# An attention kernel on one core: the identity for the first transposes made on Pool instead of loaded, and Pool's loads gated by another row

## The chip, the cores and the metric

The kernel runs on one core of a Trainium2 chip. The time is in device microseconds of that core; the number compared is the median of several executions. A profile is one more execution, taken with the hardware profiler.

The engines are named as in the profile: PE is TensorE's matmul, PEld its weight load, DVE is VectorE, ACT ScalarE, POOL GpSimd, SP SyncE. A name with a q (ACTq, SPq) is the engine's sequencer, which issues DMAs. Loads issued from SP and ACT go through one DMA queue each (q1 and q10 in the profile), loads issued from Pool through q0; all of them share the core's 16 DMA engines.

## The reference

Plain attention over 8 batches, sequence length 2048, width 512, in float32:

```python
def reference(q, k, v):
    d_k = q.shape[-1]
    scores = np.matmul(q, k.transpose(0, 2, 1)) / np.sqrt(d_k)
    attn_weights = special.softmax(scores, axis=-1).astype(np.float32)
    return np.matmul(attn_weights, v)
```

## The kernel before

The kernel computes scores transposed (keys on the partitions, 512 queries side by side), takes their exponentials into float16 and multiplies these with V; a column of ones behind V gives the row sums. Most products run through a seven-product scheme for 2x2 blocks (Q and K sums on DVE, PE accumulating in PSUM); the scheme's steps are written out by hand as word lists, one word an action, in `SEQUENCES` and `OPENING`. Each engine executes its instructions in the order in which the program names them. Batch 0 is the only one whose loads nothing hides, and the change touches only its opening.

**Rows and chunks.** Q and K of a batch are 16 rows of 128x512 (a row: 128 positions on the partitions), in four chunks of four rows. Their transposes (width on the partitions) are needed as PE operands. For batch 0 most are made on PE against an identity, `nc.tensor.transpose(..., ident)` in `transposed` (L156); a DVE or ACT copy then takes the result from PSUM (L159). Later chunks and batches use DMA transposes from SP (L146).

**The first chunk.** `load_first` (L131) loads each of the first four rows of Q and of K by itself, in float32, into space that is used for other things later (`rows`, `cz`). The queues, in order of issue: SP takes Q row 0, Q row 1, K row 1, Q row 2, K row 2, Q row 3, K row 3; ACT takes K row 0, behind the identity's load (L95). `round_first` (L135) casts each row to float16, Q rows on DVE, K rows on ACT. `first_transpose` then transposes one row on PE, and DVE copies it. `piece` (L258) multiplies what is there already. `idle` (L768) issues dummy products on a zeroed tile named `warm` (it lies in `vt2`; L709 zeroes it on DVE), which keep PE running between them.

PE's order in the opening is: 6 dummies of 512 columns; transposes of Q row 0; 2 dummies; transposes of Q row 1; 4 dummies of 128 columns; transposes of K row 0; 6 dummies of 128 columns; the first piece (K row 0 with Q row 0); transposes of K row 1; a piece; transposes of Q row 2; and so on. DVE's order is: cast and copy of Q row 0, cast and copy of Q row 1, copy of K row 0, cast of Q row 2, copy of K row 1, and so on.

**The identity.** `ident` is a 128x128 corner of the tile `vt4`, which the V sums overwrite later. Before the change it is an array in DRAM, loaded by the first instruction on ACT's queue.

**Pool.** Pool sets two columns of ones (L710, L711), then copies one column of a landed row into a tile named `gate` (L728). That copy has no use but to hold back what stands behind it on Pool: ten loads, which cast to float16 on the way. They are the other three chunks of Q and K and the four chunks of V, in this order, the first two in two halves each:

```python
LOADS = 'q1 k1 q2 k2 k3 v0 v1 q3 v2 v3'
```

The chunks k1, k2 and k3 are transposed on PE in `OPENING` (words k10s, k12v, k20v, k22s, k30s, k32s), q1 in q10v and q12v; q2 by a DMA transpose on SP (L146), which waits for q2's load.

Of the kernel before, what the change touches and what calls it, by code (L numbers as in the profile page):

```python
# [12 lines left out]
def kernel(  # L13
# [21 lines left out]
    nc = tc.nc  # L35
    P = 128
# [54 lines left out]
    vt4 = const.tile([P, NJ, H], F16, name="vt4")  # L91
    ident = vt4[:, NJ - 1, 0:P]
    warm = vt2[:, 0:2, :].rearrange("p j d -> p (j d)")
    ident_dram = nc.inline_tensor(np.eye(P, dtype=np.float16), name="attn_identity")
    nc.scalar.dma_start(out=ident, in_=ident_dram.ap())  # L95
    NK = NJ // 2
    Q = H // 2
    vus = [[const.tile([P, NK, Q], F16, name=f"vu{n}_{h}") for n in (1, 2, 4)] for h in range(2)]
# [25 lines left out]
    firsts = {}  # L124
# [582 lines left out]
    )  # L707

    nc.vector.memset(warm, 0.0)  # L709
    nc.gpsimd.memset(vt1[:, :, H:H + 1], 1.0)  # L710
    nc.gpsimd.memset(vraw[0][:, :, 1, D:D + 1], 1.0)  # L711

# [12 lines left out]
        load_first("k", n, nc.sync, rest[n])  # L725

    gate = const.tile([P, 1], F32)
    nc.gpsimd.tensor_copy(out=gate[:], in_=firsts["k", 0][:, 0:1])  # L728

    new_p(1)  # L730
    spare = [
# [153 lines left out]
```

## Time and profile before

| | us |
|---|---|
| median of 3 runs | 788.87 |
| lowest, highest | 788.74, 789.52 |
| the profiled execution | 790.05 |
| its span | 788.2 |

The profiled execution is one more run; its own time stands 1.2 us over the median, and its span leaves 1.8 us around it. The page's second part cuts the span into 40 equal slices (19.7 us each):

```profile
## 2 busy tenths in 40 slices
PE   8999999999999999999999999999999999999998
...
DVE  5799988989889898998879988799897988889884
ACT  4888788787877878878787878878788777887762
POOL 4011100011000110010100001000110001100000
...
DMA  9999895889958889589895989958898688921113
```

Each digit is a tenth of busy time. PE is full but for the first and the last slice; the DMA engines are full in the first slices and have room after that.

In the lists that follow, a row of the timeline gives start and length in us, engine, line, operation, tiles (out<-in), shapes and, in brackets, how long the engine had been idle and what ended that. The chain of waits gives start, length and what, followed back from the last instruction. A DMA row gives the tiles, the issuing queue, the KB and the time from issue to landing.

### The profile page before, as it was taken

The numbers are of one execution on the slowest core, as the hardware profiler recorded it, in microseconds if no ns is written. First come the engines' busy times: TensorE is split into PE (matmuls) and PEld (weight loads), VectorE is DVE, ScalarE is ACT, GpSimd is POOL, SyncE is SP. The second block draws the span as 40 slices with busy tenths as digits, with TensorE's granted clock in tenths as the row PEclk, the third lists the DMA queues.
The fourth block names the chain that finished last, engine by engine and source line by source line (L and its number), as shares of the span: only waits on it lengthen the run. The fifth ranks groups of instructions, "written<-read, shape, count | busy, mean of one in ns | idle before, by whom it ended". The sixth has DMA issues, their size and how long they took to land.

```text
span 788.2 us, 16289 instructions
## 1 busy us (share of the span) xinstructions
PE 782.7 (99%) x6284; PEld 536.4 (68%) x6284; DVE 683.8 (87%) x1452; ACT 609.8 (77%) x1140; POOL 72.3 (9%) x105
## 2 busy tenths in 40 slices
PE   8999999999999999999999999999999999999998
PEld 6566667667667666666666666666666766766677
DVE  5799988989889898998879988799897988889884
ACT  4888788787877878878787878878788777887762
POOL 4011100011000110010100001000110001100000
PEclk9999999999999999999999999999999999999999
DMA  9999895889958889589895989958898688921113
GB/s 210 190 155 167 155 182 125 164 149 151 198 114 162 156 150 175 110 162 179 119 193 126 160 161 146 191 108 169 141 191 155 117 178 137 191 75 45 48 67 110
DMA packets 187789, 115.90 MB, mean 147 GB/s; under 512 B 121536, under 2 KB 170816, under 8 KB 187712
## 3 DMA queue, kind: packets, MB, share of 16 engines
q0 software_dynamic: 49664, 49.29, 43.7%
q1 hardware_dynamic: 137616, 65.22, 36.8%
q8 instruction: 49, 0.80, 0.4%
q10 hardware_dynamic: 432, 0.36, 0.2%
q14 instruction: 28, 0.23, 0.1%
HBM read 100.70 MB, written 33.55 MB: 170 GB/s over the span
## 4 chain that ended last, share of the span: by engine, by line
PE 97%; DMA 2%; DVE 0%; ACT 0%; issue 0%; ACTq 0%; DVEq 0%
PE t L298 46%; PE t L494 36%; PE t L418 12%; DMA kraw<-stage 1%; PE t L243 1%; PE t L258 1%; PE tr L156 1%; DMA rows<-in_k_dram 1%; PE t L566 0%; DVE kraw L159 0%; ACT rows L435 0%; DVE rows L506 0%; DVE ks L185 0%; ACT stage L135 0%; DVE cz L318 0%
## 5 line engine op out<-in xcount | busy, mean ns | idle before, releaser
L298 PE MATMUL t<-qraw,kraw 128*128 128x512 f16 x732 | 192.4, 379 | 0.0
L494 PEld LDWEIGHTS <-s 128*128 128x128 f16 x1536 | 147.8, 98 | 39.4 <-ACT rows L503 0.3
L298 PEld LDWEIGHTS <-kraw 128*128 128x128 f16 x984 | 93.3, 98 | 79.0 <-issue 0.2
L298 PE MATMUL t<-qs,ks 128*128 128x512 f16 x492 | 141.1, 379 | 0.0
L494 PE MATMUL t<-vt,s 128*128 128x257 f16 (+1 forms) x1024 | 132.9, 273 | 0.0
L237 ACT ACTIVATE right<-cz 128x1024 f16<-128x1024 f32 x123 | 129.9, 1056 | 0.3 <-DVE cz L318 0.3
L426 DVE TENSOR_TENSOR rows<-t,rows 128x256 f32<-128x256 f32 x210 | 88.1, 419 | 22.3 <-ACT rows L517 11.8
L298 PEld LDWEIGHTS <-ks 128*128 128x128 f16 x738 | 69.3, 98 | 46.7 <-issue 0.2
L503 ACT ACTIVATE rows<-t,scales 128x256 f32<-128x256 f32 x136 | 63.9, 471 | 45.2 <-PE t L494 20.9
L506 DVE SCALAR_TENSOR_TENSOR rows<-t,scales,rows 128x256 f32<-128x256 f32 (+1 forms) x134 | 64.0, 479 | 34.4 <-ACT rows L503 21.0
L321 DVE TENSOR_TENSOR cz<-t,cz 128x512 f32<-128x512 f32 x123 | 84.2, 685 | 10.5 <-ACT cz L315 7.9
L237 ACT ACTIVATE left<-t 128x512 f16<-128x512 f32 x128 | 76.5, 598 | 20.1 <-PE t L298 16.3
L237 ACT ACTIVATE right<-t 128x512 f16<-128x512 f32 x138 | 83.1, 605 | 8.5 <-PE t L298 5.7
L318 DVE TENSOR_TENSOR cz<-t,cz 128x512 f32<-128x512 f32 x123 | 84.2, 684 | 4.4 <-PE t L298 3.8
L312 ACT COPY cz<-t 128x512 f32<-128x512 f32 x122 | 71.4, 585 | 15.7 <-PE t L298 13.5
L315 ACT COPY cz<-t 128x512 f32<-128x512 f32 x123 | 71.6, 582 | 10.3 <-PE t L298 10.0
L418 PEld LDWEIGHTS <-left 128*128 128x128 f16 x960 | 62.3, 98 | 23.3 <-DVE left L398 4.1
L308 ACT COPY t<-t 128x512 f32<-128x512 f32 x121 | 69.8, 577 | 6.3 <-PE t L298 4.0
L298 PE MATMUL t<-qraw,ks 128*128 128x512 f16 x246 | 73.2, 379 | 0.0
L298 PE MATMUL t<-qs,kraw 128*128 128x512 f16 x246 | 73.2, 379 | 0.0
L494 PE MATMUL t<-vh,right 128*128 128x256 f16 x544 | 69.8, 273 | 0.0
L494 PE MATMUL t<-vh,s 128*128 128x257 f16 x512 | 66.7, 273 | 0.1
(87 smaller groups left out, 1067.1 us busy)
## 6 DMA issues: line engine op xcount, KB each, us to landing
out_dram<-rows SPq DMA_DIRECT2D x60, 512.0 KB, 3.4
vh<-in_v_dram POOLq DMA_DIRECT2D x32, 512.0 KB, 10.8
stage<-in_q_dram POOLq DMA_DIRECT2D x28, 512.0 KB, 6.5
stage<-in_k_dram POOLq DMA_DIRECT2D x28, 512.0 KB, 7.2
right<-in_k_dram POOLq DMA_DIRECT2D x2, 512.0 KB, 12.1
out_dram<-rows SPq DMA_DIRECT2D x4, 256.0 KB, 2.0
out_dram<-rows SPq DMA_DIRECT2D x7, 128.0 KB, 1.7
rows<-in_q_dram SPq DMA_DIRECT2D x2, 256.0 KB, 3.3
```

Source lines behind the costliest of these rows:

```text
L237: nc.scalar.activation(out=out_, in_=in_, func=EXP, scale=inv_sqrt_d)
L298: nc.tensor.matmul(dst[:], lhs[:, j, dc, :], rhs[:, :, dc, :], start=(n in (1, 5) and dc == 0), stop=(dc == 1), skip_group_check=True,)
L308: self.edges[0](out=self.y[:], in_=self.x[:])
L312: self.edges[1](out=self.cz[:, 1, :], in_=self.z[:])
L315: nc.scalar.copy(out=self.cz[:, 0, :], in_=self.x[:])
L318: nc.vector.tensor_add(self.cz[:, 1, :], self.x[:], self.cz[:, 1, :])
L321: nc.vector.tensor_add(self.cz[:, 0, :], self.z[:], self.cz[:, 0, :])
L418: nc.tensor.matmul(to, lhs[:, j, h, :], rhs[:, j, :], start=(n in (1, 2) and h == 0 and j == 0), stop=(j == NK - 1), skip_group_check=True,)
L426: nc.vector.tensor_add(acc, part, acc)
L494: nc.tensor.matmul(dst[:, 0:width], lhs(j), rhs(j), start=(first and j == 0), stop=(j == NJ - 1), skip_group_check=True,)
L503: nc.scalar.activation(out=out_, in_=src, func=COPY, scale=r)
L506: nc.vector.scalar_tensor_tensor(out=out_, in0=src, scalar=r, in1=out_, op0=MULT, op1=ADD)
```

## The change

The array in DRAM and its load on ACT's queue go. Pool makes the identity instead: a memset of the 128x128 corner to zero, and a select on the index (partition minus column), which keeps the zero where the index is not zero and fills in 1 where it is. Both stand on Pool ahead of the two columns of ones, and so ahead of the gate. The gate copy reads K row 1 instead of K row 0, and so waits for that row's landing.

```diff
-    ident_dram = nc.inline_tensor(np.eye(P, dtype=np.float16), name="attn_identity")
-    nc.scalar.dma_start(out=ident, in_=ident_dram.ap())
...
     nc.vector.memset(warm, 0.0)
+    nc.gpsimd.memset(ident, 0.0)
+    nc.gpsimd.affine_select(
+        out=ident, in_=ident, compare_op=mybir.AluOpType.not_equal, fill=1.0,
+        base=0, pattern=[[-1, P]], channel_multiplier=1,
+    )
     nc.gpsimd.memset(vt1[:, :, H:H + 1], 1.0)
     nc.gpsimd.memset(vraw[0][:, :, 1, D:D + 1], 1.0)
...
     gate = const.tile([P, 1], F32)
-    nc.gpsimd.tensor_copy(out=gate[:], in_=firsts["k", 0][:, 0:1])
+    nc.gpsimd.tensor_copy(out=gate[:], in_=firsts["k", 1][:, 0:1])
```

## The prediction

> **What bounds the kernel now.** I read the page's busy times first, then the chain of work that ended last in its first 13 us, then who waits for whom on PE.
>
> ```profile
> span 788.2 us, 16289 instructions
> PE 782.7 (99%) x6284; PEld 536.4 (68%) x6284; DVE 683.8 (87%) x1452; ACT 609.8 (77%) x1140; POOL 72.3 (9%) x105
> ```
>
> PE is busy for 782.7 of 788.2 us, so anything that no PE instruction waits for is worth nothing. The list of PE's waits over the whole span has three entries:
>
> ```profile
> PE t L768 <- DVE vt L709: 1.2, 1, 1.2
> PE tr L156 <- ACT stage L135: 0.6, 1, 0.6
> PE t L258 <- DVE kraw L159: 0.2, 1, 0.2
> ```
>
> All lie in the opening. The chain shows what set their end (start, length, what):
>
> ```profile
> ...
> 1.13 5.24 DMA rows<-in_k_dram
> 6.37 0.02 issue
> 6.39 0.63 ACT stage L135
> 7.02 0.05 issue
> 7.07 0.41 PE tr L156 x4
> 7.48 0.02 issue
> 7.50 0.44 DVE kraw L159
> 7.94 0.05 issue
> 7.98 0.40 PE t L258 x4
> 8.38 0.24 PE tr L156 x4
> 8.62 0.02 issue
> 8.64 0.43 DVE kraw L159
> 9.08 0.05 issue
> 9.12 0.61 PE t L258 x4
> ```
>
> The transfer of K row 0, issued at 1.13, lands at 6.37; then come its cast on ACT and its transposes on PE. Behind 9.12 the chain is PE pieces without a pause. So this change is worth what it moves the PE stream at 9.12 by, and whatever a later load then takes back.
>
> **What is removed.** The timeline of the opening (start, length, what; in brackets the idle time before and what ended it):
>
> ```profile
> 0.73 0.37 ACTq L95 DMA_DIRECT2D vt<-attn_identity  x1
> 0.74 0.87 SPq L131 DMA_DIRECT2D rows<-in_q_dram  x2
> 1.13 0.48 ACTq L131 DMA_DIRECT2D rows<-in_k_dram  x1
> 1.66 0.42 SPq L131 DMA_DIRECT2D rows<-in_k_dram  x1
> 3.58 0.43 DVE L135 CAST stage<-rows 128x512 f16<-128x512 f32 x1 [2.45 <-DMA rows<-in_q_dram]
> 4.06 0.61 PE L156 MATMUL tr<-vt,stage 128*128 128x128 f16 x4
> 7.07 0.40 PE L156 MATMUL tr<-vt,stage 128*128 128x128 f16 x4 [0.63 <-ACT stage L135]
> ```
>
> and the landing of K row 1, from the DMA issues (KB each, us from issue to landing):
>
> ```profile
> rows<-in_k_dram SPq DMA_DIRECT2D x1, 256.0 KB, 4.9
> ```
>
> Without the identity K row 0 is issued at 0.73 instead of 1.13, 0.40 earlier, and its queue no longer has 32 KB of identity ahead of it. Q row 0, on SP's queue, takes 2.8 us from issue (0.74) to its cast (3.58), K row 0 takes 5.24. If K row 0 takes anything from 2.8 to 4.9 us (the time of K row 1), it lands between 3.5 and 5.6, is cast by 6.3 at the latest, and PE no longer waits for it: the 0.63 us of idle time before 7.07 is the most that can be won here. The 0.2 us for DVE behind it stays: it is the copy of the transposed row.
>
> **What is paid for it.** The row then competes with Q row 0, and Q row 0 starts a chain too: its cast at 3.58, its transposes at 4.06, a copy, Q row 1's cast, transposes and copy, and then, in PE's order, K row 0's transposes. Each tenth by which Q row 0 lands later takes a tenth from the 0.63. Stages of the opening (PE, PEld, DVE, ACT, POOL busy; granted clock, DMA share, GB/s):
>
> ```profile
> 2.00:2.50 0.50, 0.50 (x3) 0.21 (x2) 0.00 (x0) 0.50 (x1) 0.00 (x0) 1.00 0.39 130
> 2.50:3.00 0.50, 0.50 (x3) 0.22 (x2) 0.00 (x0) 0.42 (x1) 0.00 (x0) 1.00 1.01 357
> ```
>
> A row of 0.26 MB at 360 GB/s takes 0.72 us of all 16 engines. That is the upper bound of Q row 0's delay; the lower is 0. From 2.0 to 2.5 the engines are 0.39 busy, so 0.30 us of their time is free, and the identity's own packets go:
>
> ```profile
> q10 hardware_dynamic: 129, 0.03, 8.4%
> ```
>
> (ACT's queue from 1.0 to 2.6 us: 129 small packets, 8.4% of 1.6 us, 0.13 us.) I take 0.72 - 0.30 - 0.13 = 0.29, nearer to the low end. The term is 0.63 - 0.29 = 0.34 won; its bounds are 0.63 won and 0.09 lost.
>
> The Trainium skill's DMA: Bandwidth & Descriptors (Issuing engines are not separate DMA queues) says that DMAs of all issuing engines interleave on the same 16 DMA engines, and that issuing from several saves only the sequencer's time. By that rule the queue's room in front of K row 0 is worth its 0.40 us of issue alone and Q row 0 pays the full row, so the term would be 0.09 lost; the trace's share of 0.39 between 2.0 and 2.5 speaks against the full price.
>
> **What is added.** Pool gets a memset of 128x128 f16 and the select. Neither is in this trace. Pool's groups (busy, mean ns of one):
>
> ```profile
> L710 POOL MEMSET vt<- 128x8 f16 x1 | 0.1, 133 | 0.3 <-POOLq L869 0.3
> L869 POOL MEMSET const-float32-0.0<- 128x1 f32 x1 | 0.1, 98 | 0.2 <-issue 0.2
> ```
>
> Seven more columns cost a memset 35 ns, 5 ns a column: 0.73 us for 128. A lower bound for the select is the same 0.73; an upper one is 128 times a whole one-column memset, 128 x 0.098 = 12.5 us. I take up to 1.5 us (twice the memset, since it also reads), nearest to the column rate. From Pool's first free time, 0.73 in the trace of before, the identity is then done at 0.73 + 0.73 + 1.5 = 3.0. The first transposes need it at 4.06, so 1.1 us covers it, and more if Q row 0 comes later. PE's earliest start on K row 0 lies 7.07 - 0.63 - 4.06 = 2.38 behind the first transposes, so the identity costs nothing at the end until it is later than 7.07 - 2.38 = 4.69; beyond that it costs one for one. Behind it on Pool stand two memsets of 128x8 (0.13 each), needed much later, and the gate.
>
> **What is moved.** The gate copy on Pool waits for K row 1 instead of K row 0, and all ten loads on Pool's queue stand behind it. K row 1 landed at 1.66 + 4.9 = 6.56:
>
> ```profile
> 6.42 0.18 POOL L728 COPY gate<-rows 128x1 f32<-128x1 f32 x1 [5.52 <-DMA rows<-in_k_dram]
> 10.23 1.53 POOL L121 DMA_DIRECT2D right<-in_k_dram  x2
> right<-in_k_dram POOLq DMA_DIRECT2D x1, 512.0 KB, 11.2
> 21.81 0.61 PE L156 MATMUL tr<-vt,right 128*128 128x128 f16 x8
> ```
>
> So the gate opens 6.56 - 6.37 = 0.19 later if K row 1 keeps its time, and 0.06 later if the identity's 0.13 of DMA time is gone before it. Had the gate stayed on K row 0, it would have opened with it, earlier by about 1 to 3 us, into the rows' own traffic. Who waits for Pool's queue next: the load of K's third quarter was issued at 10.23 and landed at 10.23 + 11.2 = 21.43; PE transposes it at 21.81, 0.38 later. That cover is used from both sides: the load comes 0.06 to 0.19 later and PE 0.34 earlier. PE can win 0.38 - 0.06 = 0.32 at the most there, and 0.19 at the least, so this caps the 0.34. I take 0.26, the middle.
>
> **The sum.** The profiled execution took 790.05 us, 788.2 of it span and 1.8 around it. Span after: 788.2 - 0.26 = 787.9, with what lies around it 789.8. The three runs have a median of 788.87, 1.18 under the profiled one; the same step gives 788.87 - 0.26 = 788.6. The removed ACT issue and the other eight row loads cost nothing further: ACT's next work is the cast, and the last K and Q rows have their transposes behind PE's own work.
>
> **Rivals.**
> - *The wait moves, no gain.* Q row 0 pays the full 0.72, or Pool's queue slips by more than the 0.38 of cover (K row 1 landing 0.4 later than now, pushed by K row 0, which then no longer shares its time). For it: the engines are full from 2.5 us on. Against: 0.39 before that, and no more bytes are ahead of K row 1 than now. Price: 0.09 lost to 0 won, 788.9.
> - *The select is slow; slower than before.* Place: PE's first transposes, which then wait for Pool. It decides from 4.69 us on. For it: no Pool operation of this width is in the trace, and a one-column operation takes 98 ns (a memset) to 0.18 us (the gate copy). Against: the 5 ns a column of the memset. With the upper bound the identity is done at 0.73 + 0.73 + 12.5 = 14.0, a loss of 9.3; halfway in ratio between 1.5 and 12.5 (4.3) it is done at 5.8, a loss of 1.1; over about 4.8 the loss passes 1.58. I price the case at a select of 5.3 us: 6.8, a loss of 2.1, 791.0. The Trainium skill's GPSIMD Engine Reference (Instruction dispatch) says that the first call into a freshly loaded Pool kernel pays some 6 us with no instruction to show it; by that the identity would be done at about 7.5, and the sum would be 791.7; no run here shows whether the select is such a call.
> - *PE stays at half rate for longer.* PE starts slow (first row: the opening's first wide products; second: four such in the later chain).
>
> ```profile
> 1.19 2.74 PE L768 MATMUL t<-vt 128*128 128x512 f16 x6 [1.19 <-DVE vt L709]
> 37.17 0.86 PE t L243 x4
> ```
>
> Six products of 512 columns take 2.74, 0.46 each; four take 0.86 in the stream, 0.22 each. The rate changes between 5.5 and 7.1 (four transposes take 0.61, then 0.40). A later Q row 0 leaves PE idle longer near 4 us; if the change of rate comes behind 9.1 for it, the 1.05 us of PE work in the chain from 7.07 to 9.12 (0.41, 0.40, 0.24) takes twice as long. Price: 1.05 - 0.26 = 0.8 lost, 789.7. Against: the dummy products before and behind stay.
> - *More is won.* Q row 0 is not late and K row 1 lands early with the rest, so Pool's queue starts earlier too and caps nothing: 0.63, and at the very most the 0.2 of the third wait in PE's list as well. Price: 788.0 to 788.2.
>
> **How the numbers follow.** Chances: the forecast 0.36, the wait moves 0.15, the slow select 0.18, half rate for longer 0.12, more won 0.09; a Q row 0 that lands as late as K row 0 does now (5.24 - 2.8 - 0.63 = 1.8 lost, 790.7) 0.05, and a gain that no row here shows 0.05. What this kernel's measurement can tell from no change is about 0.2%, 1.58 us: below 787.29 or above 790.45. Forecast and "the wait moves" lie inside. The slow select is slower for 0.15 of its 0.18. Half rate lies inside but for 0.05, where the change of rate comes later still; the late Q row 0 is slower for its 0.05. More won is inside but for 0.05, since the runs shown spread by 0.78 (788.74 to 789.52), and the gain not shown is faster for its 0.05. So faster 0.10, slower 0.25, same 0.65. The range reaches down to the gain of 0.83 with half of that spread, 787.6, and up to 790.8, just past the late Q row 0 and short of the slow select as priced, whose far end is left out. The likeliest case alone has 788.2 (0.63 won) to 789.0 (0.09 lost).
>
> **What would show it.** Right: K row 0's cast starts before 5.6, the first transposes wait for Q row 0's cast and not for Pool, PE starts K row 0's transposes between 6.4 and 7.0, the gate copy starts between 6.4 and 6.6, and the PE stream stands 0.2 to 0.4 earlier at 30 us, with at most 0.1 of new waiting near 21.8. Wrong: a wait of PE for Pool at the first transposes; a Q row 0 cast behind 4.3; over 0.4 us from one product of 512 columns to the next behind 9 us; the gate behind 6.9.

## The result, and the profile after

| | before | changed |
|---|---|---|
| median of 10 runs, us | 788.93 | 790.79 |
| lowest to highest | 788.67 to 789.74 | 789.72 to 792.21 |
| the profiled execution, its span | 790.05, 788.2 | 790.73, 788.8 |

The ratio is 1.0023 (95% interval 1.0014 to 1.0031): 1.86 us slower by the medians. The two profiled executions differ by 0.7 only, because the one shown of the kernel before was itself 1.1 us over its median; a second profile of it stands under the experiments.

The page of the changed kernel, its busy times:

```profile
span 788.8 us, 16292 instructions
PE 783.1 (99%) x6284; PEld 537.4 (68%) x6284; DVE 683.7 (87%) x1452; ACT 610.2 (77%) x1140; POOL 72.3 (9%) x107
```

PE is as full as before. Its waits over the whole span (us in total, times, longest):

```profile
PE tr L154 <- DVE stage L133: 1.2, 1, 1.2
PE t L771 <- DVE vt L707: 1.2, 1, 1.2
```

The wait for K row 0's cast on ACT (0.6) is gone. In its place PE waits 1.2 us for a cast on DVE: Q row 0's. The timeline of the opening (start, length, what):

```profile
0.73 0.41 ACTq L129 DMA_DIRECT2D rows<-in_k_dram  x1
0.73 0.20 POOL L708 MEMSET vt<- 128x128 f16 x1 [0.29 <-POOLq L872]
0.74 0.87 SPq L129 DMA_DIRECT2D rows<-in_q_dram  x2
1.01 0.29 POOL L709 TENSOR_SCALAR_AFFINE_SELECT vt<-vt 128x128 f16<-128x128 f16 x1
...
4.68 0.43 DVE L133 CAST stage<-rows 128x512 f16<-128x512 f32 x1 [3.55 <-DMA rows<-in_q_dram]
4.86 0.62 ACT L133 CAST stage<-rows 128x512 f16<-128x512 f32 x1 [2.40 <-DMA rows<-in_k_dram]
...
5.16 0.61 PE L154 MATMUL tr<-vt,stage 128*128 128x128 f16 x4 [1.24 <-DVE stage L133]
...
6.09 0.18 POOL L731 COPY gate<-rows 128x1 f32<-128x1 f32 x1 [4.68 <-DMA rows<-in_k_dram]
```

Q row 0 and K row 0 are now issued in the same instant on two queues and land within 0.2 us of each other: K row 0's cast starts 1.53 earlier than in the profile shown of before (4.86 against 6.39), Q row 0's 1.10 later (4.68 against 3.58). The identity is finished at 1.30, long before anybody asks for it.

The chain of waits (start, length, what) tells the second part:

```profile
0.74 3.92 DMA rows<-in_q_dram
...
5.16 0.61 PE tr L154 x4
5.77 0.85 PE t L771 x2
...
9.22 0.43 PE tr L154 x4
9.64 0.40 PE t L256 x4
10.04 0.22 PE tr L154 x4
```

From 5.2 us on the chain is PE alone. Four transposes take 0.43 us at 9.2 and 0.22 at 10.0: PE went to its full rate only between these two. In the chain of before the first 0.24 stands at 8.38, and by the timeline the rate had changed before 7.1. The granted clock of the profile's rows reads 1.00 through these microseconds, so the half rate shows in the durations alone. The Trainium skill's TensorE: Matmul & The Clock Gate (Part 1: The HAM clock gate) has it that PE's clock is halved until a free-running window of some 3.4 us has been busy. The trace is in line with it: after 1.2 us of standing idle the change comes between 9.2 and 10.0 instead of between 5.5 and 7.1.

### The profile page after: what moved, and what is told of

It reads as the page before. It is cut to its first block, busy times and chain, and to the rows that moved or that the text cites. A ratio compares the mean times of both kernels' runs of the same rounds, so it can differ in the third digit from the quotient of the medians.

```text
span 788.8 us, 16292 instructions
## 1 busy us (share of the span) xinstructions
PE 783.1 (99%) x6284; PEld 537.4 (68%) x6284; DVE 683.7 (87%) x1452; ACT 610.2 (77%) x1140; POOL 72.3 (9%) x107
## 4 chain that ended last, share of the span: by engine, by line
PE 99%; DMA 0%; DVE 0%; issue 0%
PE t L296 47%; PE t L492 36%; PE t L416 12%; PE t L241 1%; PE t L256 1%; PE tr L154 1%; DMA rows<-in_q_dram 0%; PE t L771 0%; PE t L564 0%; DVE stage L133 0%; DVE rows L504 0%
```

## The experiments

Theory A: Q row 0 is late because K row 0, with nothing ahead of it on ACT's queue, takes DMA time from it; that costs a late start of PE and, by A1, a later change of its rate as well (A2: the late start alone). The rivals are the select (B) and the gate (C). Theory D came up on the way: with PE's opening early, Pool's loads are the bound. Medians are of 11 or 12 runs each, ratios against runs of the kernel before on the same chip. These had medians of 789.28 beside b_again, e_select, e_gate and e_sp, 789.05 beside e_cold and the two e_late_g runs, and 789.12 beside the others.

| run | median, us | ratio, 95% interval |
|---|---|---|
| b_again | 788.96 | 0.9994 (0.9986 to 1.0003) |
| e_select | 789.21 | 0.9996 (0.9987 to 1.0004) |
| e_gate | 789.15 | 0.9996 (0.9987 to 1.0004) |
| e_gate0 | 790.72 | 1.0015 (1.0006 to 1.0024) |
| e_late | 789.58 | 1.0005 (0.9996 to 1.0014) |
| e_dummy | 790.11 | 1.0009 (1.0000 to 1.0018) |
| e_cold | 789.53 | 1.0005 (0.9996 to 1.0014) |
| e_sp | 790.47 | 1.0015 (1.0005 to 1.0025) |
| e_spq1 | 790.24 | 1.0013 (1.0003 to 1.0022) |
| e_late_g0 | 789.33 | 1.0005 (0.9996 to 1.0014) |
| e_late_gq0 | 789.20 | 1.0007 (0.9998 to 1.0015) |

**b_again: the kernel before, a second profile.**

> The kernel before once more, for a second profile of it and as a control. All theories: ratio 1.000 within 0.001. Open is whether its profiled opening repeats: Q row 0's cast at 3.6 us, K row 0's at 6.4, PE's rate change between 5.5 and 7.1, and whether the profiled execution again stands about 1 us over the median.

The timing repeats, the opening doesn't. Its ACT and PE rows:

```profile
5.28 0.62 ACT L135 CAST stage<-rows 128x512 f16<-128x512 f32 x1 [2.37 <-DMA rows<-in_k_dram]
5.97 0.40 PE L156 MATMUL tr<-vt,stage 128*128 128x128 f16 x4 [0.72 <-DVE stage L135]
6.43 0.39 PE L156 MATMUL tr<-vt,stage 128*128 128x128 f16 x4
8.48 0.61 PE L258 MATMUL t<-qraw,kraw 128*128 128x256 f16 x4
```

K row 0 is cast at 5.28, not 6.39, and PE starts its transposes at 6.43 with no idle time before them (no bracket). It waits for Q row 1 instead (0.72, at 5.97), whose load on SP's queue the change doesn't touch. The piece that the chain of before had at 9.12 starts at 8.48; the changed kernel starts it at 10.16, 1.68 later, close to the 1.86 between the medians. From there on the distance stays: the last products of the kernel start at 784.63 in the changed kernel and at 783.09 in b_again, 1.54 apart. So between these two profiles the whole loss arises in the first 10 us. The profiled execution was 789.00. So the 0.63 us of waiting for K row 0 belonged to the one execution shown; here there was none to win. The execution shown of before was also late a second time: PE stands 0.6 behind b_again until 365 us and 1.0 behind it at 398, and in between its chain goes through a transposing DMA of K (11.07 us, from 376.79). The opening is only part of what it was over its median.

**e_select and e_gate: one part of the change alone.** Both are shown against the kernel before.

```diff
-    nc.scalar.dma_start(out=ident, in_=ident_dram.ap())
+    nc.scalar.dma_start(out=vt4[:, NJ - 2, 0:P], in_=ident_dram.ap())
...
+    nc.gpsimd.memset(ident, 0.0)
+    nc.gpsimd.affine_select(out=ident, in_=ident, ...)
```

> The select makes the identity, but the 32 KB load stays ahead of K row 0 on ACT's queue (into a corner of vt4 that nobody reads before the V sums overwrite it); the gate is the old one. Theory A (K row 0 with nothing ahead of it takes DMA time from Q row 0): as before, 788.9 +- 0.3, Q row 0's cast at 3.6 and no PE wait of 1.2 us at the first transposes. Theory B (the select itself costs): 790.0 to 790.8. Theory C (the gate): as before.

```diff
-    nc.gpsimd.tensor_copy(out=gate[:], in_=firsts["k", 0][:, 0:1])
+    nc.gpsimd.tensor_copy(out=gate[:], in_=firsts["k", 1][:, 0:1])
```

> The kernel before with the gate moved to K row 1, nothing else. Theory A and theory B: as before, 788.9 +- 0.3, the gate opening 0 to 0.6 us later and PE's opening unchanged. Theory C (moving the gate costs, since Pool's loads then start at another time): 790.0 to 790.8.

Neither can be told from before. With the 32 KB load left in its place Q row 0's cast starts at 3.67 (e_select); with the gate moved alone it opens at 5.71, and no cost shows (e_gate). Theory B falls, and C as far as the gate alone goes.

**e_gate0: the changed kernel with the old gate.**

> The changed kernel with the gate back on K row 0 (landing near 4.8). Theory A: PE is late by itself and waits for no load of Pool's, so the time stays at 790.8 +- 0.4; at the most Pool's loads, now starting 1.2 us earlier, slow the last rows. Theory C (the gate is the cost): 789.3 or below.

790.72: undoing the gate gives nothing back. In its profile the first transposes' wait is put down to the gate copy on Pool, but they start 0.05 behind the end of Q row 0's cast (5.20 to 5.63), the usual step.

**e_late: K row 0 held back, with no transfer in front of it.**

```diff
+    nc.scalar.copy(out=scales[:, 0, 0, 0:1], in_=warm[:, 0:1])
     load_first("k", 0, nc.scalar, row(1))
```

> The changed kernel with one tiny copy on ACT (of the zeroed dummy tile, into a column of scales that nobody reads) ahead of K row 0's issue, so that this is issued at 2.0 to 2.4 instead of 0.73, with no transfer in front of it. Theory A (only the sharing of Q row 0's first microseconds costs, whatever stands there): Q row 0's cast at 3.4 to 3.7, K row 0's at 5.3 to 6.4, 788.9 +- 0.4. Rival (it was the identity's packets that helped, by warming something up): Q row 0's cast stays behind 4.3 and the time near 790.8.

The copy delays the issue less than expected: K row 0 is issued at 1.17, not at 2.0 to 2.4; in the kernel before it was 1.13. That is enough. Q row 0's cast is back at 3.68, K row 0's starts at 5.04, and most of the loss is gone (789.58 against 790.79). It was not the identity's packets that helped, but that K row 0 was issued 0.4 later. Why the median stays 0.46 over that of before beside it (789.12; the ratio's interval includes 1) may lie in PE's timeline:

```profile
21.45 0.62 PE L154 MATMUL tr<-vt,right 128*128 128x128 f16 x8 [0.34 <-DMA right<-in_k_dram]
...
24.52 0.62 PE L154 MATMUL tr<-vt,right 128*128 128x128 f16 x8 [0.27 <-DMA right<-in_k_dram]
```

PE now stands early (0.2 ahead of b_again at 20 us) and waits for the third and fourth quarter of K, whose loads stand behind the gate (open at 6.01 here, at 5.31 in b_again). But this profile is of an execution of 790.13, 0.55 over the median; how much such waits cost in the others isn't shown.

**e_dummy and e_cold: PE's rate by itself.** e_dummy has the late Q row 0 with PE kept busy (`idle(5)` becomes `idle(8)` in the changed kernel); e_cold has Q row 0 on time with PE idle (`idle(5)` becomes `idle(2)` in the kernel before).

> The changed kernel with three more dummy products of 512 columns (8 instead of 5 in the second group), which fill PE's wait for Q row 0. Theory A1 (the late Q row 0 costs twice: about 1 us of late start, and PE's rate change one stretch of 3.4 us later because PE stood idle): the rate change comes before 8 us, and the time falls by 0.5 to 0.9 from 790.8, to about 790.1. Theory A2 (the late start alone): 790.8 +- 0.3.

> The kernel before with three dummy products of 512 columns fewer (2 instead of 5 in the second group), so that PE stands idle for 1.3 us more ahead of Q row 0, which lands on time. Theory A1 (idle time ahead of the first transposes by itself puts off PE's rate change): the rate change comes 3.4 us later in part or all of the executions, and the time rises by 0.4 to 0.9 from 789.1, to about 789.7. Theory A2 (only the late start counts): 789.1 +- 0.2.

e_dummy's chain:

```profile
5.10 0.44 DVE stage L133
5.54 0.05 issue
5.58 0.41 PE tr L154 x4
```

Q row 0 is later still than in the changed kernel (cast at 5.10), but PE is at its full rate when the row comes: the four transposes take 0.41 where they took 0.61. 0.68 us come back by the medians. The traces have the same: from the start of K row 0's transposes to that of the piece that stood at 9.12 in the chain of before it takes 2.05 us in both profiles of before and in e_dummy (7.30 to 9.35), and 2.70 in the changed kernel (7.46 to 10.16), 0.65 more at half rate; e_select and e_gate, where the rate changes near 7, stand between with 2.29. e_cold is the counterpart, its PE timeline:

```profile
4.31 0.61 PE L156 MATMUL tr<-vt,stage 128*128 128x128 f16 x4 [1.66 <-DVE stage L135]
...
8.15 0.63 PE L156 MATMUL tr<-vt,stage 128*128 128x128 f16 x4
```

Q row 0's cast starts at 3.82, and yet four transposes still take 0.63 at 8.15. The median rises by 0.48 over that of before beside it (789.05), the side and size that A1 expected; the interval of the ratio includes 1, so the time alone would not show it. The profiled execution, 790.35, is the slowest of the eleven, so the late change of rate need not have come in all of them.

**e_sp and e_spq1: all rows on SP's queue.** K row 0 goes second on SP's queue, behind Q row 0; in e_spq1 the gate copy also reads Q row 1.

```diff
-    load_first("k", 0, nc.scalar, row(1))
+    load_first("k", 0, nc.sync, row(1))
```

> The changed kernel with K row 0 issued on SP's queue, second behind Q row 0, so that the rows go one after the other. Theory A: Q row 0's cast comes back to 3.4 to 3.7, PE's wait at the first transposes goes from 1.2 to under 0.2 us, and the time falls to 788.9 or below (788.0 to 789.0). Theories B and C: 790.5 to 791 stays.

> The changed kernel with K row 0 on SP's queue second behind Q row 0, and the gate on Q row 1 (third in that queue, landing near 5.2) instead of K row 1 (near 6.5). Theory D (in that order PE's opening is the earliest of all, and what took the gain back was the late gate: K's third quarter landing at 21.3 and PE waiting for it): PE's waits at 21 and 42 us shrink from 0.4 and 0.2 to under 0.1 and the time falls from 790.5 to 788.2 to 788.9. Theory E (rows on one queue are slow in themselves): 790 or more stays.

Q row 0's cast comes back as theory A expected (3.46 and 3.66), but neither time comes down. In its profiled execution (789.66, 0.8 under the median) e_sp has its gate open at 6.57, and PE waits for K's third quarter:

```profile
21.33 0.62 PE L154 MATMUL tr<-vt,right 128*128 128x128 f16 x8 [0.21 <-DMA right<-in_k_dram]
```

In e_spq1 the row that now stands third is late:

```profile
6.47 0.40 PE L154 MATMUL tr<-vt,stage 128*128 128x128 f16 x4 [1.47 <-DVE stage L133]
```

These are Q row 1's transposes; its cast starts at 5.99 (5.05 and 5.49 in the two profiles of before). The wait moves from one row to the next. What makes the median of e_sp 790.47, and single executions go up to 792.13, stays open: no trace of such an execution is there.

**e_late_g0 and e_late_gq0: e_late with an earlier gate.** The gate copy reads K row 0, or Q row 0.

> The changed kernel with K row 0 issued behind a tiny copy on ACT (as in e_late) and the gate back on K row 0 (landing near 5.0 instead of K row 1's 6.0). Theory D (with PE's opening early, Pool's loads are the bound: K's third and fourth quarter landed at 21.4 and 24.5 in e_late and PE waited 0.3 us for each): the loads land about 0.8 earlier, those waits go, and the time falls from 789.6 to 788.2 to 788.8, below the kernel before. Rival (the gate is not what those loads wait for, since the DMA engines are full): 789.3 to 789.9 stays.

> As e_late_g0, with the gate on Q row 0 (landing near 3.6). Theory D: Pool's loads land earlier still, but their packets now share the engines with K rows 1 to 3 and Q rows 2 and 3; the last rows' casts move from 8.6 to 9.5 or later and PE's opening loses 0.3 to 1.0, so 788.5 to 789.5. Rival: 789.3 to 789.9 as in e_late.

Theory D's waits go, but its price doesn't come. e_late_g0 opens the gate at 4.95 and PE's list has no wait for K's quarters any more:

```profile
PE t L772 <- DVE vt L707: 1.2, 1, 1.2
PE t L256 <- DVE kraw L157: 0.2, 1, 0.2
```

but the median falls by 0.25 only, to 789.33, and the interval of its ratio to the kernel before includes 1. With the gate open at 3.61 (e_late_gq0) ACT's last row cast starts at 9.06 instead of 8.81, less than expected, and the time is the same again. No version tried here beats the kernel before.

## Why the prediction was wrong

The time is inside the range by 0.01 only (790.79, the upper end is 790.8), and on the other side than the forecast: 1.9 lost instead of 0.3 won. It is also past 790.45, beyond which the prediction saw a chance of 0.25. One of its signs of being wrong came true: Q row 0's cast behind 4.3. By its steps:

- **What is removed** held as far as K row 0 goes: its cast starts before 5.6 (4.86), and PE no longer waits for it. But the 0.63 us to be won came from one profiled execution 1.1 us over the median. In b_again, e_select and e_gate K row 0 is cast at 5.05 to 5.28, in time, and there the term is nothing.
- **What is paid for it** is the step that failed. It gave Q row 0 a delay of 0.29, between 0 and 0.72; measured are 1.10 (cast at 3.58, then 4.68), and 1.5 to 1.6 in the profiles of e_dummy and e_gate0, against 3.6 to 3.7 in b_again, e_select and e_gate. The way the term was counted held: against the profile that it was worked out from, 0.63 - 1.10 makes 0.47 lost, and K row 0's transposes start 0.39 later (7.46 against 7.07). The bound priced a row at the steady 360 GB/s and counted idle DMA engines as room. The windows of the changed kernel (last columns: granted clock, DMA share, GB/s):

```profile
2.00:2.50 0.50, 0.50 (x3) 0.21 (x2) 0.00 (x0) 0.46 (x1) 0.00 (x0) 1.00 0.78 180
2.50:3.00 0.50, 0.50 (x3) 0.22 (x2) 0.00 (x0) 0.00 (x0) 0.00 (x0) 1.00 0.75 197
3.00:3.50 0.50, 0.50 (x3) 0.02 (x1) 0.00 (x0) 0.00 (x0) 0.00 (x0) 1.00 1.02 242
3.50:4.00 0.50, 0.42 (x1) 0.00 (x0) 0.00 (x0) 0.00 (x0) 0.00 (x0) 1.00 0.98 373
```

  From 2.5 to 3.0 the engines moved 357 GB/s in the profile shown of before, nearly all of it for SP's queue, which has Q row 0; with both rows issued in the same instant they move 197 at a share of 0.75, and the queues halve it (from 2 to 3 us):

```profile
q10 hardware_dynamic: 43, 0.09, 39.0%
q1 hardware_dynamic: 49, 0.10, 37.4%
```

  SP's queue, with Q row 0, moved 0.10 MB in that microsecond. In the profile shown of before it was

```profile
q1 hardware_dynamic: 113, 0.22, 57.7%
```

  A full row at 190 GB/s is 1.4 us by estimate, the size of the delays measured (1.10 to 1.62), where the term's upper bound was 0.72. Why two rows together move less than one is not shown. The Trainium skill's rule on issuing engines (DMA: Bandwidth & Descriptors, Issuing engines are not separate DMA queues), that their DMAs interleave on the same 16 engines, agrees with the trace (39.0% and 37.4% of the engines for the two queues in the same microsecond), and rightly spoke against the change; the 0.09 lost that the prediction worked out with it had the same wrong rate.
- **What is added** was right: memset 0.20, select 0.29, the identity done at 1.30 where 3.0 was allowed. The rival of a slow select falls. The 6 us that the Trainium skill's GPSIMD Engine Reference (Instruction dispatch) has for a first call into a freshly loaded kernel don't show: the select starts 0.28 behind the start of the memset and is done by 1.30.
- **What is moved**: the gate opened at 6.09, earlier than the 6.4 to 6.6 expected. The cover of K's third quarter did not matter, since PE was late; where PE is early (e_late), the cap is there, with 0.3 of waiting at 21.5 and at 24.5.
- **The rival of half rate** had the right mechanism and a chance of 0.12; the forecast's sum had no term for it. Its price, 0.8 net, stood on top of a forecast gain. By e_dummy the later change of rate is worth 0.7 of the 1.86 by the medians; the rest, about 1.2, is the late start: Q row 0's 1.1 with nothing to set against it. The traces divide it much the same: K row 0's transposes start 1.03 later than in b_again (7.46 against 6.43), and the half rate adds 0.65 up to the piece at 10.16, together the 1.68 by which it stands behind b_again. These are single executions, and the ratios' intervals are 0.002 wide, so the parts are known to some tenths.
- **The rival of a Q row 0 as late as K row 0 is now** (1.8 lost, 790.7, chance 0.05) comes nearest by its number, but by luck: the cast came 1.1 later, not 1.8, and the half rate made up the rest.

## What to carry to other kernels

An issue that stands in front of another on a queue can be what keeps the second transfer from taking bandwidth when the first row of all needs it (here 0.4 us of issuing was enough): before removing it, ask what then starts at the same instant on the other queues. Price early transfers by the rate that the first microseconds show with several rows in flight, not by the steady one. And when a gain is a wait of half a microsecond in one profile, take a second profile first: here the wait was that execution's own.

## What was not expected of the hardware

In the changed kernel the rate at which the first rows come was half the later one although the engines were busy: 180 to 197 GB/s at shares of 0.75 to 0.78 between 2 and 3 us, 373 GB/s between 3.5 and 4.0. The other profiles bear it out: between 2.5 and 3.0 us it is 197 to 213 GB/s in the three in which K row 0 and Q row 0 are issued in the same instant (the changed kernel, e_gate0, e_dummy), and 274 to 403 in the ten others.

And standing idle in the opening left PE at half rate for longer in these profiles. In the three in which PE stands idle for 1.24 to 1.76 us in front of Q row 0's transposes, four products of 128 columns still take 0.6 behind 9.0, whether the row is late (the changed kernel, e_gate0) or not (e_cold). In the ten others, with at most 0.51 us idle there, they take 0.4 by 7.9 at the latest, in e_dummy by 5.6.
